# The down projection of a gated conv-MLP as seven quarter products per pair of contraction chunks, in a hybrid decoder layer on one core

## The chip, the core and the metric

The kernel runs on one core of a Trainium2 chip. The metric is the device time of one execution in microseconds (us); the median of three runs of the kernel before is 1024.78 us, the lowest 1024.64 and the highest 1025.79. The engines are named as in the profile: PE is TensorE (PEld its weight load), DVE is VectorE, ACT is ScalarE, POOL is GpSimd, SP is SyncE, which issues most transfers.

## The reference, cut to what matters

One decoder layer on 512 tokens of width 1024, in float32: a recurrent mixer and an attention mixer, merged and added to the residual stream, then a gated conv-MLP. The change is in the last line, the product with `w_down` (3072 x 1024).

```python
D_MODEL, SEQ = 1024, 512
D_FF, FFN_CONV_W = 3 * D_MODEL, 3
...
        x = x + (jax.nn.sigmoid(mg_rnn) * y_rnn + jax.nn.sigmoid(mg_attn) * y_attn) @ w_out
        up = causal_dwconv(rms_norm(x, norm2_g) @ w_up, ffn_conv_w, ffn_conv_b)
        gate, val = jnp.split(up, 2, axis=-1)
        x = x + (jax.nn.gelu(gate) * val) @ w_down
```

## The kernel before

Activations lie with the channels on the 128 partitions and the 512 tokens along the free axis. Every operand of a product is split in two, a rounded high part and the remainder as low part, and each product is three matmuls: high by high, high by low, low by high. For a weight tile of 128 x 1024, `_wprep` (line 141) issues the load into `wraw` on SP, lets ACT round it into `whi` (line 169) and DVE subtract to get `wlo` (line 177); while the attention heads run (`pool_lo`), POOL does that subtraction instead, in four pieces of 256 columns (line 174). `PLAN` lists all weight tiles in the order of their use, and `w` (line 194) prepares up to `ahead` further ones; `whi` and `wlo` have three buffers each.

The order of TensorE's work is written out by hand in the attention heads and in the MLP; what the other engines do is put in order by the scheduler, as their inputs and buffers are expected to come free.

The MLP is `ffn` (line 1255). Its up projection has 2 x 24 chunks of 128 channels. The first `NPL` = 6 pairs (a gate chunk and a value chunk) are plain products (`plain`). The other 18 are done as two-by-two blocks with seven quarter products instead of eight (`seed`, line 1329, and `rest`, line 1350): each quarter product `prod` (line 1320) is 4 x 3 matmuls with 256 columns. The sums of activation blocks are made once (`prep`); the sums of weight blocks are made in DRAM by `sums` (line 1223): SP copies blocks of the weights into a DRAM tile `ws`, and three transfers that add to what is there, issued on POOL's queue (line 1237), form the sums. `_wprep` moves `sums` on by a step each time that the position in `PLAN` has grown by the step in `SUM_RATE`, so this work is spread over the whole program. A chunk pair ends with the convolution (`conv`: one ACT operation and two on DVE), the Gelu on ACT, and the product of gate and value on POOL (`gated`, line 1278), which gives one of 24 chunks of `f`, 128 x 512.

The down projection is `down` (line 1383). For each of the 24 chunks k, `get` (line 1389) prepares the weight tile 128 x 1024 and splits the chunk of `f` into `fh` and `fl`; then, for each of the eight output blocks m, `mm3` (line 203) does three matmuls with 512 columns into the block's PSUM bank. The last two chunks are done block by block, with the residual added on DVE and the block stored as it is ready; the last block in two halves (line 1423 and 1424). It uses no POOL instruction and no weight sum.

Of the kernel before, what the change touches and what calls it, by code (L numbers as in the profile page):

```python
# [74 lines left out]
def weight_plan():  # L75
# [23 lines left out]
    p += [("dn", c, 1024) for c in range(24)]  # L99
# [21 lines left out]
class Kern:  # L121
# [18 lines left out]

    def _wprep(self, i, rp=None, pri=None):
# [3 lines left out]
        if name == "w2":  # L145

            raw = self.ea.tile([128, n], F32, name="w2r")
            hi, lo = (self.wp.tile([128, 1024], F32R, name=t, bufs=3) for t in ("whi", "wlo"))
        else:
            raw, hi, lo = self.wtiles(rp or more, more is None)  # L150
        w = self.a["w"][i, :, :n]
        if name in ("u1", "u2", "u3"):
            while self.sum_done < c:
# [14 lines left out]
        with self.tc.high_priority(self.wpri if pri is None else pri):  # L168
            self.last_hi = nc.scalar.copy(hi[:, :n], raw[:, :n])  # L169
            if self.pool_lo and (name, c) not in DVE_LO:  # L170
# [1052 lines left out]
    def sums(self):  # L1223
# [12 lines left out]
        def add(j, o, src):  # L1236
            nc.gpsimd.dma_start(self.ws[j][o], src, accum_op=ALU.add, max_dma_last_dim=8192)  # L1237
# [16 lines left out]

    def ffn(self):
# [27 lines left out]
        ff.tile([128, 8], F32, name="opad")  # L1283

        def op(name, src):
            SB[name] = [ff.tile([128, 4, 256], F32R, name=name + h) for h in ("h", "l")]
# [86 lines left out]
        ff.tile([128, 56], F32, name="fpad")  # L1373
        with self.tc.tile_pool(name="fd", bufs=1, reuse_waits="tile") as fd:
            self.rp2 = fd
            part = seed(NPL)
# [4 lines left out]
            self.down(fd, fs)

    def down(self, fd, fs):

        nc = self.nc
        ps = [self.ps.tile([128, S], F32, name="mm", bufs=self.mmb) for _ in range(7)]
        ps.append(self.ps.tile([128, S], F32, name="misc"))
        ops = {}
        def get(k):
            w = self.w("dn", k, 2 if k < 2 else 1)  # L1390
            h, l = (fd.tile([128, S], F32R, name=n, bufs=4) for n in ("fh", "fl"))
            nc.scalar.copy(h, fs(k))

            with self.tc.issue_after(self.last_sum.ins):
                nc.vector.tensor_sub(l, fs(k), h.bitcast(F32))
            ops[k] = (w, (h, l))

        def mm(m, k, c=slice(0, S)):
            w, x = ops[k]
            self.mm3(ps[m][:, c], w, slice(128 * m, 128 * m + 128), [t[:, c] for t in x], k == 0, k == FC - 1 and c.stop == S)  # L1400


        get(0)
        get(1)
        for ms in (range(0, 4), range(4, 8)):
            for k in range(2):
                for m in ms:
                    mm(m, k)
        for k in range(2, FC - DLAST):
            get(k)  # L1410
            for m in range(8):
                mm(m, k)
        for k in range(FC - DLAST, FC):
            get(k)
# [173 lines left out]
```

## Time and profile before

| what | value |
|---|---|
| runs | 1024.64, 1024.78, 1025.79 us |
| span of the profiled execution | 1024.1 us |
| attention heads, 75 to 350 us | PE busy 271.67 of 275, POOL 109.65, DMA share 0.47 |
| quarter products of the up projection, 713 to 889 us | PE and PEld busy 176.00 of 176, DVE 147.70, POOL 26.07, DMA share 0.67 |
| down projection, 889 to 1020 us | PE 131.00 of 131, PEld 108.72, DVE 49.31, ACT 36.06, POOL 2.90, DMA share 0.28 |

The time of the profiled execution itself is not given beside its span. The span goes from its first to its last instruction; the runs of the same kernel take 0.5 to 1.7 us more. Busy shares count an instruction from its start to its modelled end; matmuls overlap one another, so a rate of matmuls is read from the distance between their starts. An instruction of DVE or POOL that waits for a memory port is shown as running: its duration then is longer than that of its like.

### The profile page before, as it was taken

To read this page: it belongs to the slowest core of one execution; us is meant where nothing else is said; L and a number is where in the kernel's file an instruction comes from. 1 tells how busy PE (TensorE), PEld (TensorE's weight loads), DVE (VectorE), ACT (ScalarE), POOL (GpSimd) and SP (SyncE) were. 2 spreads that over 40 slices of the span, in tenths; PEclk is the share of its full clock that TensorE was granted. 3 is DMA by queue.
4 is the path that set the end of the run, shared out by engine and by line. 5 is a ranking of instruction groups with operands and counts; after the bars stand their busy time and mean duration, and the time that the engine had idled before them with its cause. 6 is when DMAs were issued, how large, how long until landed. Compare 5 with 4: busy or idle time off the path is not lost.

```text
span 1024.1 us, 15686 instructions
## 1 busy us (share of the span) xinstructions
PE 1013.5 (99%) x5663; PEld 882.2 (86%) x5663; DVE 750.7 (73%) x1443; ACT 615.3 (60%) x1023; POOL 243.8 (24%) x316
## 2 busy tenths in 40 slices
PE   9999999999999999999999999999999999999998
PEld 7888888988878888888888888888999999988887
DVE  6868879788878687679598564599788888933333
ACT  6466776868777663588788533365566666533320
POOL 0155334234433300342332014222211111100000
PEclk9999999999999999999999999999999999999999
DMA  7523453454545567765432987656966566632312
GB/s 252 112 89 105 124 124 116 120 120 109 145 103 150 144 218 220 218 199 165 138 92 88 291 234 208 173 151 209 266 207 200 176 194 192 200 102 85 102 62 82
DMA packets 63166, 160.88 MB, mean 157 GB/s; under 512 B 16299, under 2 KB 17963, under 8 KB 60208
## 3 DMA queue, kind: packets, MB, share of 16 engines
q1 hardware_dynamic: 57040, 137.92, 40.5%
q0 software_dynamic: 5904, 21.81, 12.6%
q8 instruction: 44, 0.72, 0.3%
q14 instruction: 34, 0.28, 0.1%
q10 hardware_dynamic: 144, 0.15, 0.0%
HBM read 150.63 MB, written 44.04 MB: 190 GB/s over the span
## 4 chain that ended last, share of the span: by engine, by line
PE 85%; DVE 8%; ACT 4%; issue 1%; DMA 1%; POOL 0%; SPq 0%; DVEq 0%; ACTq 0%
PE mm L206 16%; PE mm L207 16%; PE mm L208 16%; PE mm L1325 6%; PE mm L1326 6%; PE mm L1327 6%; PE O L916 4%; PE T L925 3%; PE S L885 1%; PE S L886 1%; PE v L767 1%; ACT s L896 1%; PE mm L1173 1%; PE em L382 1%; PE em L206 1%
## 5 line engine op out<-in xcount | busy, mean ns | idle before, releaser
L169 ACT CAST whi<-wraw 128x1024 fp32r<-128x1024 f32 (+2 forms) x202 | 203.3, 1006 | 223.9 <-PE misc L207 76.9
L177 DVE TENSOR_TENSOR wlo<-wraw,whi 128x1024 fp32r<-128x1024 f32 (+2 forms) x169 | 196.2, 1161 | 131.5 <-ACT whi L169 131.3
L206 PE MATMUL mm<-xh,whi 128*128 128x512 f32 x456 | 178.7, 392 | 0.0
L208 PE MATMUL mm<-xh,wlo 128*128 128x512 f32 x456 | 178.4, 391 | 0.0
L207 PE MATMUL mm<-xl,whi 128*128 128x512 f32 x456 | 178.2, 391 | 0.0
L174 POOL TENSOR_TENSOR wlo<-wraw,whi 128x256 fp32r<-128x256 f32 (+1 forms) x131 | 95.3, 781 | 131.9 <-ACT whi L169 110.6
L208 PEld LDWEIGHTS mm<-xh,wlo 128*128 128x128 f32 x456 | 85.6, 188 | 18.6
L206 PEld LDWEIGHTS mm<-xh,whi 128*128 128x128 f32 x456 | 85.6, 188 | 16.7
L207 PEld LDWEIGHTS mm<-xl,whi 128*128 128x128 f32 x456 | 85.6, 188 | 16.7
L896 ACT ACTIVATE s<-s,bs,rq 128x128 f32<-128x128 f32 (+3 forms) x128 | 82.5, 648 | 19.1 <-DVE bs L893 19.1
L232 DVE TENSOR_TENSOR ptl<-T,pth 128x512 fp32r<-128x512 f32 x80 | 55.1, 688 | 17.9 <-ACT pth L231 17.0
L207 PE MATMUL mm<-fl,whi 128*128 128x512 f32 x168 | 65.4, 389 | 0.0
L206 PE MATMUL mm<-fh,whi 128*128 128x512 f32 x168 | 65.4, 389 | 0.0
L208 PE MATMUL mm<-fh,wlo 128*128 128x512 f32 x168 | 65.4, 389 | 0.0
L231 ACT CAST pth<-T 128x512 fp32r<-128x512 f32 x80 | 46.3, 583 | 28.9 <-PE T L925 28.2
L889 DVE CUSTOM_DVE_ANT_0 s<-S,cc 128x128 f32<-128x128 f32 (+3 forms) x128 | 58.0, 482 | 2.2 <-PE S L886 1.7
L1237 POOL DMA_DIRECT2D ws<-ws x36 | 28.5, 792 | 121.7 <-DMA ws<-in_wi 44.7
L925 PE MATMUL T<-cc,s 128*128 128x128 f32 x320 | 48.2, 273 | 0.6 <-DVE s L901 0.6
L925 PEld LDWEIGHTS T<-cc,s 128*128 128x128 f32 x320 | 39.5, 140 | 10.1 <-DVE s L901 0.8
L1269 DVE SCALAR_TENSOR_TENSOR y<-mm,pp,y 128x511 f32<-128x511 f32 (+1 forms) x60 | 44.4, 744 | 0.1
L916 PE MATMUL O<-pth,v 128*128 128x512 f32 (+3 forms) x128 | 42.9, 353 | 1.2 <-ACT pth L231 1.1
L901 DVE TENSOR_SCALAR s<-s,sm 128x128 f32<-128x128 f32 (+3 forms) x105 | 41.6, 442 | 1.1
(405 smaller groups left out, 2634.0 us busy)
## 6 DMA issues: line engine op xcount, KB each, us to landing
wraw<-in_w SPq DMA_DIRECT2D x126, 512.0 KB, 3.6
ws<-in_wi SPq DMA_DIRECT2D x36, 512.0 KB, 5.1
wraw<-ws SPq DMA_DIRECT2D x72, 256.0 KB, 3.2
wraw<-in_w SPq DMA_DIRECT2D x54, 256.0 KB, 3.2
ws<-in_wa POOLq DMA_DIRECT2D x18, 512.0 KB, 6.0
ws<-ws POOLq DMA_DIRECT2D x36, 256.0 KB, 4.6
xr<-in_x SPq DMA_DIRECT2D x16, 256.0 KB, 4.4
x<-in_x SPq DMA_DIRECT2D x8, 256.0 KB, 4.3
```

The costliest lines, as they stand in the source:

```text
L169: self.last_hi = nc.scalar.copy(hi[:, :n], raw[:, :n])
L174: nc.gpsimd.tensor_sub(lo[:, e], raw[:, e], hi[:, e].bitcast(F32))
L177: nc.vector.tensor_sub(lo[:, :e], raw[:, :e], hi[:, :e].bitcast(F32))
L206: nc.tensor.matmul(ps, wh, xh, start=first, stop=False)
L207: nc.tensor.matmul(ps, wh, xl, start=False, stop=False)
L208: nc.tensor.matmul(ps, wl, xh, start=False, stop=last)
L896: self.last_exp = nc.scalar.activation(s[t, x], s[t, x], AF.Exp, bias=bs[:, x, t:t + 1], scale=rq[:, t], accum_out=sm[:, x, t:t + 1])
L916: nc.tensor.matmul(O[:, q0:S], lhsT, r, start=first[0], stop=(last and n == len(rhs) - 1))
L925: nc.tensor.transpose(T[:, off:off + 128], s[i, x][:, 128 * j:128 * j + 128], self.ident)
L1325: nc.tensor.matmul(ps, w[0][:, c], xh, start=start and k == 0, stop=False, skip_group_check=True)
L1326: nc.tensor.matmul(ps, w[0][:, c], xl, start=False, stop=False, skip_group_check=True)
L1327: nc.tensor.matmul(ps, w[1][:, c], xh, start=False, stop=(k == 3), skip_group_check=True)
```

## The change

The down product is done for pairs of chunks (`pair`: k and k + 4), each a two-by-two block problem: two chunks by two halves of the 1024 outputs for the weights, two chunks by two halves of the 512 tokens for `f`. Seven quarter products instead of eight are accumulated over all twelve pairs, in two phases. In phase one (`one`, weight tiles d1 and d2) four of the products are accumulated for all twelve pairs; then `mix` combines the PSUM banks of each group (ACT copies a bank, DVE does four additions of 256 columns); in phase two (`two`, tiles d3 and d4, the latter of 512 columns) the remaining three are added. Each quarter product of a group p of output blocks is three matmuls with 256 columns; there are four groups.

The weights of a pair need four blocks that are sums. Two of them are made in DRAM by `sums`, which gets twelve more rounds behind the old ones: one copy of 512 KB on SP and two adding transfers of 256 KB on POOL's queue each. The other two are made on POOL in SBUF (`down_sums`). The activations need two differences and sums in phase one (`down_ops`: two operations on DVE, one on POOL) and one in phase two (`down_ops2`), written over chunks of `f`. `SUM_RATE` gets smaller steps, so that sums are issued closer together. The low part of d4 is made on POOL (line 205 of the new file), the others on DVE. Buffers of the up projection's operands (`fo`) are taken over as they come free.

The diff, cut to its core:

```diff
+def pair(n):
+    k = 8 * (n // 4) + n % 4
+    return k, k + 4
-SUM_AT, SUM_RATE = 20, ((43, 1.0), (66, 2.4), (82, 16.0), (116, 2.0), (999, 3.0))
+SUM_AT, SUM_RATE = 20, ((43, 0.6), (66, 1.5), (82, 16.0), (116, 1.3), (999, 2.4))
...
-    p += [("dn", c, 1024) for c in range(24)]
+    for n in range(FC // 2):
+        p += [("d1", n, 1024), ("d2", n, 1024)]
+    for n in range(FC // 2):
+        p += [("d3", n, 1024), ("d4", n, 512)]
...
+    def dtiles(self, i):
+        if (i - WIDX[("d1", 0)]) % 4 == 3:
+            return [self.fo.tile([128, 1080 - o], F32R, name=t, tag=g)[:, 56 - o:1080 - o]
+                    for t, g, o in (("whi", "t4h", 0), ("wlo", "t4l", 56))]
+        return [self.wp.tile([128, 1024], F32R, name=t, bufs=3) for t in ("whi", "wlo")]
...
+            m = c + FC // 2 * (name == "d3")
+            if name in ("d1", "d3") and m:
+                self.down_load(m + 2)
+                self.down_sums(m + 1)
+            raw = self.dn_raw.pop((name, c))
+            hi, lo = self.dtiles(i)
...
-            if self.pool_lo and (name, c) not in DVE_LO:
+            if (self.pool_lo and (name, c) not in DVE_LO) or name == "d4":
...
+        for n in range(N + 2):
+            if n < N:
+                self.ds[n] = self.drp.tile([64, 2048], F32, name=f"dn{n}")
+                nc.sync.dma_start(self.ds[n], a["wd"][n])
+                yield
+            if 0 <= n - 1 < N:
+                add(self.ds[n - 1][0:32], a["we"][n - 1])
+            if 0 <= n - 2 < N:
+                add(self.ds[n - 2][32:64], self.ds[n - 2][0:32])
+            yield
...
+    def down_load(self, m):
...
+            if late:
+                dma(g[:, 512:], w[i, :, 512:1024])
+                dma(g[:, 0:512], self.dsum(n, 1))
+                dma(s[:, 0:512], w[i + 1, :, 0:512])
+            else:
+                dma(g[:, 0:512], w[i, :, 0:512])
+                dma(s[:, 0:512], w[i, :, 512:1024])
+                dma(g[:, 512:], self.dsum(n, 1))
+                dma(s[:, 512:], self.dsum(n, 0))
...
+    def down_sums(self, m):
...
+            if late:
+                self.nc.gpsimd.tensor_tensor(g[:, 0:512], g[:, 0:512], g[:, 512:], ALU.add)
+            else:
+                self.nc.gpsimd.tensor_tensor(s[:, 0:512], s[:, 0:512], g[:, 0:512], ALU.add)
...
+    def down_ops(self, n, fs):
...
+        v.tensor_sub(t[:, 0], b11, b12)
+        nc.gpsimd.tensor_tensor(t[:, 1], b22, b12, ALU.subtract)
+        v.scalar_tensor_tensor(b12, t[:, 0], -1.0, b22, ALU.mult, ALU.subtract)
+        self.split(flat(h[:, 0:2]), flat(l[:, 0:2]), f1)
+        self.split(flat(h[:, 2:4]), flat(l[:, 2:4]), flat(t))
...
+    def down_ops2(self, n, fs):
...
+        v.scalar_tensor_tensor(f1[:, 0:256], f1[:, 256:512], -1.0, f2[:, 0:256], ALU.mult, ALU.subtract)
+        self.split(flat(h[:, 0:2]), flat(l[:, 0:2]), f2)
+        self.split(h[:, 2], l[:, 2], f1[:, 0:256])
...
+            nc.tensor.matmul(ps, w[0][:, c], x[0][:, i], start=start, stop=False, skip_group_check=True)
+            nc.tensor.matmul(ps, w[0][:, c], x[1][:, i], start=False, stop=False, skip_group_check=True)
+            nc.tensor.matmul(ps, w[1][:, c], x[0][:, i], start=False, stop=stop, skip_group_check=True)
...
+        get1(0)
+        for p, which in ((0, "ac"), (1, "ac"), (2, "c"), (0, "de"), (1, "de"), (2, "ade")):
+            one(p, 0, which)
+        get1(1)
+        for p, n in ((0, 1), (1, 1), (3, 0), (2, 1), (3, 1)):
+            one(p, n)
+        for n in range(2, N):
+            get1(n)
+            for p in range(4):
+                one(p, n)
+                if n == N - 1:
+                    mix(p)
...
+        for p in range(3):
+            two(p, N - 1)
+            store(p, 0, (slice(0, S),))
+            store(p, 1, (slice(0, S),))
+            if p < 2:
+                two(p + 2, N - 2)
+        for s in "cda":
+            two(3, N - 1, s)
+            if s == "c":
+                store(3, 1, (slice(0, S),))
+        store(3, 0, (hi, lo))
```

How the change moves instructions is shown at three places. TensorE's order is the same up to the first matmul of the down product, and everything behind that is new. In the middle of the down product, DVE's order before is this: `wlo` is the low part of a weight tile, `fl` that of a chunk of `f`, for one chunk after the other.

```order
L177 TENSOR_TENSOR wlo_10177<-wraw_10175,whi_10176 128x1024
L1395 TENSOR_TENSOR fl_10250<-fxl_7329,fh_10249 128x512
L177 TENSOR_TENSOR wlo_10211<-wraw_10209,whi_10210 128x1024
L1395 TENSOR_TENSOR fl_10284<-fxl_7329,fh_10283 128x512
L177 TENSOR_TENSOR wlo_10245<-wraw_10243,whi_10244 128x1024
```

DVE's order now, for one pair in the middle of phase one (`dg` and `ds` are the raw tiles d1 and d2, `dt` the differences of blocks of `f`, `dl` the low parts of the activation operands):

```order
L208 TENSOR_TENSOR wlo_10159<-dg_10005,whi_10158 128x1024
L208 TENSOR_TENSOR wlo_10163<-ds_10006,whi_10162 128x1024
L263 TENSOR_TENSOR dl_10289<-fxh_7388,dh_10288 128x512
L263 TENSOR_TENSOR dl_10289<-dt_10287,dh_10288 128x512
L1501 SCALAR_TENSOR_TENSOR fxh_7388<-fxh_7388 128x256
L1487 TENSOR_TENSOR dt_10505<-fxl_7389 128x256
L1489 SCALAR_TENSOR_TENSOR fxl_7389<-dt_10505,fxl_7389 128x256
```

A pair now has two weight tiles, two splits and three small operations, one of which (line 1501) belongs to phase two. Each of the seven has two inputs, both in SBUF.

POOL's last instructions before are the products of gate and value of the last chunks:

```order
L1278 TENSOR_TENSOR fxl_7329<-y_9240,y_9245 128x512
L1278 TENSOR_TENSOR fxl_7329<-y_9370,y_9375 128x512
L1278 TENSOR_TENSOR fxl_7329<-y_9500,y_9505 128x512
L1278 TENSOR_TENSOR fxl_7329<-y_9629,y_9634 128x512
L1278 TENSOR_TENSOR fxl_7329<-y_9687,y_9692 128x512
```

Now, from the product of chunk 21 on, POOL's order runs like this, with the weight sum `ds` (line 1329) and the difference `dt` (line 1488) of the first pairs among them:

```order
L1354 TENSOR_TENSOR fxl_7389<-y_9560,y_9565 128x512
L1329 TENSOR_TENSOR ds_9780<-ds_9780,dg_9779 128x512
L1488 TENSOR_TENSOR dt_9922<-f0_6931 128x256
L1488 TENSOR_TENSOR dt_10068<-fxh_7388 128x256
L1354 TENSOR_TENSOR fxl_7389<-y_9689,y_9694 128x512
L1329 TENSOR_TENSOR ds_9797<-ds_9797,dg_9796 128x512
L1354 TENSOR_TENSOR fxl_7389<-y_9755,y_9760 128x512
L1329 TENSOR_TENSOR ds_9848<-ds_9848,dg_9847 128x512
L1488 TENSOR_TENSOR dt_10141<-fxh_7388 128x256
```

Behind that come one `ds` and one `dt` per pair, and in phase two one sum of 512 columns (line 1327) and two low parts of 256 columns (line 205) per pair.

In the attention heads POOL also issues the adding transfers. Before, between low parts of weights (line 174) and operations of the compressed attention (lines 834 to 865), where `ws` is the DRAM tile of the sums:

```order
L1237 DMA ws6_1326<-ws6_1326 32x2048 x2
L174 TENSOR_TENSOR wlo_1481<-wraw_1479,whi_1480 128x256 x4
L1237 DMA ws7_1761<-in_wa 64x2048
L174 TENSOR_TENSOR wlo_1599<-wraw_1597,whi_1598 128x256 x4
L174 TENSOR_TENSOR wlo_1759<-wraw_1757,whi_1758 128x256 x4
L1237 DMA ws7_1761<-ws7_1761 32x2048 x2
L174 TENSOR_TENSOR wlo_1936<-wraw_1934,whi_1935 128x256 x4
L1237 DMA ws8_2356<-in_wa 64x2048
```

The same stretch of POOL's order now:

```order
L1268 DMA ws6_1326<-ws6_1326 32x2048
L1268 DMA ws7_1601<-in_wa 64x2048
L1268 DMA ws6_1326<-ws6_1326 32x2048
L205 TENSOR_TENSOR wlo_1481<-wraw_1479,whi_1480 128x256 x4
L1268 DMA ws7_1601<-ws7_1601 32x2048 x2
L205 TENSOR_TENSOR wlo_1599<-wraw_1597,whi_1598 128x256 x4
L205 TENSOR_TENSOR wlo_1761<-wraw_1759,whi_1760 128x256 x4
L1268 DMA ws8_1940<-in_wa 64x2048
L1268 DMA ws8_1940<-ws8_1940 32x2048
L205 TENSOR_TENSOR wlo_1937<-wraw_1935,whi_1936 128x256 x4
L1268 DMA ws8_1940<-ws8_1940 32x2048
```

Among the weights of the heads, POOL issues adds for 13 chunks where it did for 8 before; the twelve new rounds stand between the recurrent mixer and the first quarter products of the up projection.

More of the change, by code (lines that the diff above doesn't have):

```diff
@@ L1255, in ffn @@
+    def down_sums(self, m):
+        n, late = m % (FC // 2), m // (FC // 2)
+        if late < 2:
+            g, s = (self.dn_raw[(k, n)] for k in (("d3", "d4") if late else ("d1", "d2")))
+            if late:
+                self.nc.gpsimd.tensor_tensor(g[:, 0:512], g[:, 0:512], g[:, 512:], ALU.add)
+            else:
+                self.nc.gpsimd.tensor_tensor(s[:, 0:512], s[:, 0:512], g[:, 0:512], ALU.add)
     def ffn(self):
@@ L1281, in ffn @@
         SB = {}
[L1283 to L1286 removed]
+        FO = ExitStack()
+        tp = lambda name, **kw: self.tc.tile_pool(name=name, bufs=1, reuse_waits="tile", **kw)
+        for _ in range(4):
+            ff.tile([128, S], F32, name="y", bufs=4)
+        fo = self.fo = FO.enter_context(tp("fo"))
+        fo.tile([128, 8], F32, name="opad")
+        def op(name, src):
+            if name == "t4":
+                sizes = ((name + "h", 1080, 0), (name + "l", 1032, 8))
+                SB[name] = [fo.tile([128, n], F32R, name=t)[:, o:o + 1024].rearrange("p (k c) -> p k c", k=4)
+                            for t, n, o in sizes]
+            else:
+                SB[name] = [fo.tile([128, 4, 256], F32R, name=name + h) for h in ("h", "l")]
             self.split(*SB[name], src)
@@ L1359, in rest @@
             gated(j, yg, conv(r1, FC + j, True))
-        with self.tc.tile_pool(name="xt", bufs=1, reuse_waits="tile") as xt:
+        with tp("xt", side="right") as xt:
             x = xt.tile([128, KO, S], F32, name="xs")
@@ L1378, in ffn @@
                 nx = seed(j + 1) if j + 1 < FC else None
+                if j == FC - 3:
+                    for _ in self.sum_steps:
+                        pass
+                    self.down_load(0)
+                if nx is None:
+                    self.down_sums(0)
+                    first = self.down_ops(0, fs)
+                    fd.tile([128, 56], F32, name="fdpad")
                 rest(j, *part)
                 part = nx
[L1381 to L1414, printed above, removed]
-        for m in range(8):
@@ new lines, in ffn @@
+            self.down(fs, first)
+        FO.close()
+    def down_ops(self, n, fs):
+        nc, v = self.nc, self.nc.vector
+        k1, k2 = pair(n)
+        f1, f2 = fs(k1), fs(k2)
+        b11, b12, b22 = f1[:, 0:256], f1[:, 256:512], f2[:, 256:512]
+        t = self.dtile(n, [128, 2, 256], F32, "dt", ("t2l", "b22l"))
+        h, l = (self.dtile(n, [128, 4, 256], F32R, x, y) for x, y in (("dh", ("t1h", "b21h")), ("dl", ("t1l", "b21l"))))
+        flat = lambda x: x.rearrange("p a c -> p (a c)")
+        v.tensor_sub(t[:, 0], b11, b12)
[3 more added lines that the diff above has]
+        self.split(flat(h[:, 2:4]), flat(l[:, 2:4]), flat(t))
+        return h, l
@@ new lines, in down @@
+        get2(1)
+        for p, n in ((0, 1), (3, 0), (1, 1), (2, 1), (3, 1)):
+            two(p, n)
+        for n in range(2, N - 2):
+            get2(n)
+            for p in range(4):
+                two(p, n)
+        get2(N - 2)
+        two(0, N - 2)
+        two(1, N - 2)
+        get2(N - 1)
+        for p in range(3):
+            two(p, N - 1)
[3 more added lines that the diff above has]
+                two(p + 2, N - 2)
@@ L1525, in lay_out @@
         wa[j] = np.stack([v[:, 0:4], v[:, 4:8]])
+    wd = np.asarray(i["w_down"]).reshape(FC, 128, 2, 512)
+    ks = np.array([pair(n) for n in range(FC // 2)])
+    wd, we = np.stack([wd[ks[:, 0], :, 1], wd[ks[:, 0], :, 0]], 1), wd[ks[:, 1], :, 1]
     pp = np.zeros((128, NP_), f)
```

124 lines of the change are left out of this document (105 added, 19 removed).

## Prediction, made before the change was run

> **What bounds the kernel now.** First the busy times on the page, then the same by stage: the heads, the quarter products of the up projection, the down projection. The columns of a stage are busy time (and instructions) of PE, PEld, DVE, ACT and POOL, granted clock, DMA share and GB/s.
>
> ```profile
> PE 1013.5 (99%) x5663; PEld 882.2 (86%) x5663; DVE 750.7 (73%) x1443; ACT 615.3 (60%) x1023; POOL 243.8 (24%) x316
> 75.00:350.00 275.00, 271.67 (x1581) 235.60 (x1580) 227.75 (x688) 201.74 (x460) 109.65 (x148) 1.00 0.47 126
> 713.00:889.00 176.00, 176.00 (x1510) 176.00 (x1509) 147.70 (x216) 110.88 (x143) 26.07 (x22) 1.00 0.67 205
> 889.00:1020.00 131.00, 131.00 (x587) 108.72 (x585) 49.31 (x57) 36.06 (x47) 2.90 (x2) 1.00 0.28 92
> ```
>
> PE has no gap in the down projection and runs at full clock; everything else there is far from busy. So the stage is worth its matmuls, and the rate of matmuls is read from PE's timeline, by the distance of starts:
>
> ```profile
> 888.30 0.28 PE L1325 MATMUL mm<-t4h,whi 128*128 128x256 f32 x1
> ...
> 889.00 0.28 PE L1325 MATMUL mm<-t4h,whi 128*128 128x256 f32 x1
> ...
> 889.35 0.39 PE L206 MATMUL mm<-fh,whi 128*128 128x512 f32 x1
> ...
> 985.25 0.39 PE L206 MATMUL mm<-fh,whi 128*128 128x512 f32 x1
> ...
> 999.53 0.39 PE L206 MATMUL mm<-fh,whi 128*128 128x512 f32 x1
> ...
> 1019.89 0.28 PE L208 MATMUL misc<-fh,wlo 128*128 128x256 f32 x1
> ```
>
> Six matmuls of 256 columns take 0.70 us, 0.1167 each; 63 of 512 take 14.28, 0.2267 each. A half-size matmul is a little more than half as long.
>
> **The matmuls.** Removed are 570 of 512 columns and 12 of 256: 129.2 + 1.4 = 130.6 us, which fits the start at 889.35 and the last matmul at 1019.89. Added are 12 pairs x 4 groups x 7 products x 3 = 1008 of 256 columns: 117.6. The term is **-13.0 us**; at half of 0.2267 it would be 16.3. Phase one is 12 x 48 matmuls, 5.60 us a pair; phase two 12 x 36, 4.20 a pair. All else is what keeps PE from this pace.
>
> **The work beside it.** Prices on DVE come from its timeline at the end of the up projection and, for 256 columns, from the group of its additions there; POOL's from the products of gate and value and from a low part in the heads:
>
> ```profile
> L1344 DVE TENSOR_TENSOR ac<-mm,ad 128x256 f32<-128x256 f32 x9 | 3.8, 427 | 4.1 <-PE mm L1327 4.1
> 876.97 1.22 DVE L177 TENSOR_TENSOR wlo<-wraw,whi 128x1024 fp32r<-128x1024 f32 x1
> 878.10 0.75 DVE L1269 SCALAR_TENSOR_TENSOR y<-mm,pp,y 128x510 f32<-128x510 f32 x1
> 878.76 0.74 DVE L1269 SCALAR_TENSOR_TENSOR y<-mm,npw,y 128x511 f32<-128x511 f32 x1
> 879.42 0.68 DVE L177 TENSOR_TENSOR wlo<-wraw,whi 128x512 fp32r<-128x512 f32 x1
> 880.02 0.74 DVE L1269 SCALAR_TENSOR_TENSOR y<-mm,npw,y 128x510 f32<-128x510 f32 x1
> L1278 POOL TENSOR_TENSOR fxh<-y x8: 1297/1300/1300, 753.7 to 822.1; 128x512 f32<-128x512 f32 x8
> 353.25 2.82 POOL L174 TENSOR_TENSOR wlo<-wraw,whi 128x256 fp32r<-128x256 f32 x4 [5.49 <-ACT whi L169]
> 900.23 1.05 ACT L169 CAST whi<-wraw 128x1024 fp32r<-128x1024 f32 x1 [1.15 <-PE misc L207]
> 901.18 0.62 ACT L1392 CAST fh<-f 128x512 fp32r<-128x512 f32 x1
> ```
>
> In a row without waits an operation costs DVE the distance to the next start: 1.13 for 1024 columns, 0.60 for 512, 0.66 for a tap of the convolution; for 256, recorded at 0.43, I take 0.34, the same 0.09 less. On POOL 512 columns take 1.30 and 256 take 2.82 / 4 = 0.71.
>
> A pair of phase one needs, on DVE, 2 x 1.13 + 2 x 0.60 + 3 x 0.34 = 4.48 us of the 5.60; on ACT, 2 x 1.05 + 2 x 0.62 = 3.34; on POOL, 1.30 + 0.71 = 2.01. One of phase two: DVE 1.13 + 0.60 + 0.34 = 2.07 of the 4.20, POOL 1.30 + 2 x 0.71 = 2.72, ACT less than in phase one. Loads are 1 MB in 5.60 us and 0.75 MB in 4.20, about 187 GB/s, where the up projection moves 205 at a share of 0.67. The buffers of raw tiles let a load start two pairs ahead of its sum. Each engine alone keeps up; I cost loads and ACT at nothing.
>
> **DVE and POOL together.** They do not run freely beside each other. Six places of the timelines of POOL and DVE, and the spread of one small DVE operation (min/median/max in ns):
>
> ```profile
> 703.98 1.29 POOL L1278 TENSOR_TENSOR f<-y 128x512 f32<-128x512 f32 x1 [7.73 <-DVE y L1269]
> 704.34 2.02 DVE L177 TENSOR_TENSOR wlo<-wraw,whi 128x1024 fp32r<-128x1024 f32 x1
> 693.37 2.14 POOL L1278 TENSOR_TENSOR f<-y 128x512 f32<-128x512 f32 x1 [4.18 <-DVE y L1269]
> 693.14 1.21 DVE L177 TENSOR_TENSOR wlo<-wraw,whi 128x1024 fp32r<-128x1024 f32 x1
> 276.24 3.11 POOL L174 TENSOR_TENSOR wlo<-wraw,whi 128x256 fp32r<-128x256 f32 x4
> 276.30 3.08 DVE L893 SCALAR_TENSOR_TENSOR bs<-mx,rq 128x4 f32<-128x4 f32 x1
> L893 DVE SCALAR_TENSOR_TENSOR bs<-mx,rq x32: 153/166/3080, 88.9 to 344.5; 128x4 f32<-128x4 f32 x32
> 871.10 1.30 POOL L1278 TENSOR_TENSOR fxl<-y 128x512 f32<-128x512 f32 x1 [8.50 <-DVE y L1269]
> 871.42 0.43 DVE L1344 TENSOR_TENSOR ac<-mm,ad 128x256 f32<-128x256 f32 x1 [0.46 <-PE mm L1327]
> ```
>
> A DVE subtraction of two SBUF tiles that starts inside a POOL product ends 1.09 us after it (706.36 against 705.27), 2.02 instead of 1.22. The other way round POOL waits: it ends 1.16 after DVE (695.51 against 694.35). A DVE operation of 0.17 us lasts 3.08 through four of POOL's. An addition with one input in PSUM is not slowed at all. So operations with two inputs in SBUF take turns with POOL, and every steady operation of the new down product is such a one. A POOL operation between two of DVE puts them apart by 1.16 + 1.09 - 1.13 = 1.12 instead of its 1.30; for 256 columns I take 0.18 less too, 0.53.
>
> Phase one then needs 4.48 + 1.12 + 0.53 = 6.13 of 5.60 a pair: 0.53 too much in pairs 3 to 9, 3.7 us; pairs 10 and 11 have one small operation left and fit. That is a bound on DVE's pace and it moves PE, which waits for `wlo` of the next pair. Between all turns hidden (0) and every operation at its recorded length (2 x 1.22 + 2 x 0.68 + 3 x 0.43 + 2.01 = 7.10, 1.50 too much, 10.5 us) I take 3.7, as its rows show the turns themselves.
>
> The start: DVE's order from the first addition of the last `seed` (in this trace at 881.22) to the low part of pair 2's second tile has 7 operations of 1.13, 5 of 0.60, 8 taps of 0.66 and 9 of 0.34: 19.3 us, ending at 900.5. PE wants that part two pairs, two products and two matmuls into the stage: 889.35 + 11.2 + 0.7 + 0.2 = 901.5. One us is to spare, and POOL has seven of 512 columns and three of 256 in that time, 9.4 us in turns; 12 of DVE's operations read PSUM and take 6.6 us in which they cost nothing. Between 0 and 8.4 I take **2.3**: a third of POOL's turns delaying DVE, less the spare. Phase one: 3.7 + 2.3 = **+6.0**.
>
> Phase two needs 2.07 + 1.12 + 2 x 0.71 - 0.18 = 4.43 of 4.20: 0.23 x 11 = 2.5. The sums there are made up to two pairs ahead, so the first pairs don't feel it; I take half, **+1.2** (0 to 9.4: at recorded lengths 1.22 + 0.68 + 0.43 + 2.72 = 5.05, 0.85 too much in each).
>
> The change of phase: `mix` of the last group can't start before that group's products; its five steps, 0.6 on ACT and four of 0.34 to 0.43, stand in DVE's queue behind the other groups' and a `wlo`. PE does three groups of pair 0 and one of pair 1 ahead of it, 4.2 us. DVE's queue for that time has some 4.8: **+0.7** (0 to 2).
>
> The end, before, and a stretch of the table by stage in which the transfers run fast:
>
> ```profile
> 0.00:25.00 25.00, 23.48 (x94) 18.77 (x94) 17.43 (x31) 17.68 (x29) 0.20 (x4) 1.00 0.72 248
> 1018.77 0.69 DVE L1423 TENSOR_TENSOR y<-mm,xn 128x512 f32<-128x512 f32 x1 [0.67 <-PE mm L208]
> 1020.20 0.76 DVE L1423 TENSOR_TENSOR y<-misc,xn 128x256 f32<-128x256 f32 x2 [0.74 <-PE misc L208]
> ```
>
> DVE ends 0.8 us after PE. Now the last 18 matmuls, 2.1 us, finish four blocks, 3 x 0.60 + 2 x 0.34 = 2.5 us on DVE starting 0.9 us into them: 1.2 us after PE, 0.4 later. Three blocks of 256 KB and two halves are stored 0.6 us apart instead of 1.36; at 248 GB/s one takes 1.06, a queue of about 0.7. **+1.1** (0.4 to 2).
>
> The adds in DRAM: they touch PE only where POOL or the transfers run out. In the heads:
>
> ```profile
> L1237 POOL DMA_DIRECT2D ws<-ws x16 | 12.6, 786 | 46.4 <-DMA ws<-ws 15.6 <-DMA ws<-in_wi 11.9 <-DMA ws<-in_wa 7.7
> L1237 POOL DMA_DIRECT2D ws<-in_wa x8 | 6.9, 860 | 29.5 <-DMA ws<-in_wi 23.7 <-PE T L925 5.8
> POOL wlo L174 <- ACT whi L169: 63.0, 17, 14.0
> ```
>
> 24 adds cost POOL (19.5 + 75.9) / 24 = 4.0 us each, waits included; 15 more cost 60. POOL has 63 us there in which it waits for ACT to round a weight: that hides them, just. I take 0 (-1 to +6).
>
> **Sum.** Against the span: 1024.1 - 13.0 + 6.0 + 1.2 + 0.7 + 1.1 = 1020.1. The median run lies 0.7 above the span: **1020.8 us**.
>
> **Rivals.** (1) The turns cost nothing: POOL's operations fall into gaps of DVE, or DVE goes first and the sums are early enough. For: DVE has 1.1 us free in each pair of 5.60, and sums stand a pair ahead. Against: 4.48 and 1.65 don't fit into 5.60. Time: 1024.8 - 13.0 + 0.7 + 1.1 = 1013.6, up to 1016 with some start. 0.28.
>
> (2) Slower: DVE and POOL hold the port for the whole recorded length of each operation. By the sums above: start 8.4, phase one 10.5, phase two 9.4, with 1.8 for change and end: 1024.8 - 13.0 + 30.1 = 1042. It turns the gain into a loss once start and turns take more than 11.2 us together. For: the operation that waited 3.08 us through four of POOL's, so a run of one engine isn't broken into. Against: 1.09 and 1.16 after the other's end are less than 1.22 and 1.30. 0.10. The Trainium skill, SBUF — State Buffer, "Who interferes with whom", has this rule: a VectorE instruction with two SBUF inputs and a GpSimd instruction that reads SBUF exclude each other through a shared read port, for the whole instruction. By that rule no part of an operation overlaps, and the down product comes out at this rival's price; the trace agrees on who waits, and shows 0.13 us less of each wait.
>
> (3) POOL's queue in the heads runs full: the 60 us of waits don't fall where POOL is idle, and a low part comes late by up to one add, 4.0 us. One such wait takes the forecast's whole gain of 4.0, and that is the point from which it decides; fifteen more adds with 1.5 such waits in all cost 6: 1026.8. Against: PE loses 3.3 of 275 us in the stage now. 0.10.
>
> **How the numbers follow.** The forecast has 0.52. A measurement of this kernel can tell about 0.2%, 2.1 us, from no change: 1022.7 to 1026.8. Of the forecast's 0.52, 0.38 lie below, 0.13 within, 0.01 above; rival 1 is faster; rival 2 slower; rival 3 half within, half above. Faster 0.66, same 0.18, slower 0.16. The range reaches down to rival 1, a little under it for a DVE that ends no later, and up past rival 3: 1012.5 to 1028; rival 2 and some edges are left out.
>
> **What would show it.** Right: matmuls 0.1167 apart; DVE subtractions in the down product of 1.5 to 2.3 us beside POOL's sums; waits of PE for `wlo` of 5 to 8 us by the end of phase one, fewer in phase two. Rival 1: DVE at its old lengths and PE without gaps. Rival 2: DVE and POOL busy nearly all of the stage, and PE waiting in every pair. Rival 3: PE waits for POOL's low parts between 75 and 350 us. The forecast is wrong if PE's waits in the down product are under 3 or over 12 us, or lie before 889 us.

## The result, and the profile after

The changed kernel takes 1037.64 us (median of 4 runs, 1034.42 to 1041.22), the kernel before 1025.28 (4 runs, 1024.64 to 1026.74): ratio 1.012, interval 1.009 to 1.0151. It is slower, by 0.9 to 1.5%, and outside the range that was forecast. The profiled execution took 1034.42 us, with a span of 1032.6.

The page's busy times and the table by stage (heads, quarter products of the up projection, phase one and phase two of the new down product; columns as before):

```profile
PE 1009.4 (98%) x6089; PEld 896.8 (87%) x6089; DVE 823.3 (80%) x1531; ACT 644.8 (62%) x1075; POOL 350.7 (34%) x400
75.00:350.00 275.00, 271.24 (x1573) 234.63 (x1572) 226.96 (x690) 202.13 (x461) 118.19 (x160) 1.00 0.61 160
713.00:893.00 180.00, 180.00 (x1528) 179.34 (x1528) 154.76 (x224) 113.20 (x146) 34.94 (x28) 1.00 0.64 200
893.00:972.00 79.00, 74.55 (x598) 73.17 (x597) 75.25 (x97) 41.58 (x58) 44.21 (x24) 0.96 0.49 157
972.00:1028.00 56.00, 51.11 (x415) 50.02 (x413) 43.75 (x43) 24.37 (x41) 38.16 (x31) 0.97 0.42 138
```

In phase one DVE is now busy in 75.25 of 79.00 us, in a stage where it had been idle most of the time; PE has gaps, and in both phases the mean granted clock is below 1.00. PE's timeline shows where the down product begins, its longest wait and what follows that, and its last matmul:

```profile
893.01 0.28 PE L1521 MATMUL mm<-dh,whi 128*128 128x256 f32 x1
...
917.77 0.28 PE L1522 MATMUL mm<-dl,whi 128*128 128x256 f32 x1
920.89 0.58 PE L1523 MATMUL mm<-dh,wlo 128*128 128x256 f32 x1 [2.85 <-DVE wlo L208]
921.27 0.42 PE L1521 MATMUL mm<-dh,whi 128*128 128x256 f32 x1
921.49 0.42 PE L1522 MATMUL mm<-dl,whi 128*128 128x256 f32 x1
...
926.82 0.41 PE L1523 MATMUL misc<-dh,wlo 128*128 128x256 f32 x1
...
1027.67 0.28 PE L1523 MATMUL mm<-dh,wlo 128*128 128x256 f32 x1
```

The first down matmul starts at 893.01, where it had been 889.35: 3.7 us are lost ahead of the changed product. From the first to the last it takes 134.7 us instead of 130.5. After the last, 4.9 us remain instead of 4.2. That is the whole difference of the spans: 3.7 + 4.1 + 0.7 = 8.5.

The 1008 matmuls at 0.1167 us would take 117.5 to the start of the last, so 17.2 us are lost inside. By phase, each distance of starts less 0.1167 summed: 9.5 us in phase one, 7.6 in phase two with the change of phase. A new item is in both. Between 921.27 and 926.82 the starts are 0.2135 us apart, not 0.1167, and the granted clock of that stretch is half:

```profile
920.30:927.10 6.80, 6.21 (x29) 6.21 (x30) 6.80 (x12) 0.63 (x2) 1.04 (x2) 0.50 0.46 157
```

So a wait of 2.85 us is followed by 28 matmuls at half speed, 2.7 us more. A second one follows the longest wait of phase two and costs 1.6. These are the waits of PE from 713 us on, all of them in the down product:

```profile
PE mm L1523 <- DVE wlo L208: 4.6, 5, 2.9
PE mm L1523 <- POOL wlo L205: 3.9, 2, 2.6
PE misc L1521 <- DVE misc L1553: 0.7, 1, 0.7
```

Three places explain most of it. The **first** is the wait of 2.85 us. POOL's last product of gate and value, 1.30 us of work, is recorded with 10.84; then DVE, which until 911.90 had run one two-input operation behind the other, waits 3.13 us for POOL's activation difference, which had stood behind that product. POOL's row, then DVE's:

```profile
902.22 10.84 POOL L1354 TENSOR_TENSOR fxl<-y 128x512 f32<-128x512 f32 x1 [0.37 <-ACT y L1444]
```

```profile
911.22 0.68 DVE L263 TENSOR_TENSOR dl<-dt,dh 128x512 fp32r<-128x512 f32 x1
915.03 1.50 DVE L1489 SCALAR_TENSOR_TENSOR fxh<-dt,fxh 128x256 f32<-128x256 f32 x1 [3.13 <-POOL dt L1488]
```

After the wait DVE meets the turns of POOL that had piled up: its four operations of 256 columns from 915.03 on take 4.60 us up to the next low part, where four distances of 0.34 make 1.36. The low parts of the first weight tile show the pace of DVE over the whole phase; these are those of the first, the fifth and the ninth pair:

```profile
892.85 1.22 DVE L208 TENSOR_TENSOR wlo<-dg,whi 128x1024 fp32r<-128x1024 f32 x1
...
919.63 1.21 DVE L208 TENSOR_TENSOR wlo<-dg,whi 128x1024 fp32r<-128x1024 f32 x1
...
945.09 1.22 DVE L208 TENSOR_TENSOR wlo<-dg,whi 128x1024 fp32r<-128x1024 f32 x1
```

The first four pairs take DVE 26.8 us and the next four 25.5, where PE needs 22.4 for four; the three rows after that take 4.9 us each and fit. PE is 5.2 us behind its pace when the wait of 2.85 us ends, and loses 4.2 more in the pairs from there on, half clock included.

The **second** is at the beginning of phase two. POOL makes the sums (L1327) and the low parts of the fourth weight tile (L205) in turn; SyncE's queue issues the loads (L1313 the fourth tile's, L1311 and L1312 the third's). First POOL's timeline, then the queue's:

```profile
964.97 1.98 POOL L1327 TENSOR_TENSOR dg<-dg 128x512 f32<-128x512 f32 x1 [1.63 <-DMA dg<-dn]
966.90 2.09 POOL L205 TENSOR_TENSOR wlo<-ds,whi 128x256 fp32r<-128x256 f32 x2
973.61 1.81 POOL L1327 TENSOR_TENSOR dg<-dg 128x512 f32<-128x512 f32 x1 [4.61 <-DMA dg<-dn]
975.37 1.60 POOL L205 TENSOR_TENSOR wlo<-ds,whi 128x256 fp32r<-128x256 f32 x2
981.44 1.27 POOL L1327 TENSOR_TENSOR dg<-dg 128x512 f32<-128x512 f32 x1 [4.47 <-DMA dg<-dn]
```

```profile
962.22 7.13 SPq L1313 DMA_DIRECT2D ds<-in_w  x2
969.40 0.42 SPq L1311 DMA_DIRECT2D dg<-in_w  x1
969.87 0.43 SPq L1312 DMA_DIRECT2D dg<-dn  x1
977.00 0.33 SPq L1313 DMA_DIRECT2D ds<-in_w  x1
977.37 0.43 SPq L1311 DMA_DIRECT2D dg<-in_w  x1
```

The low part ends at 968.99 and frees a buffer; only then the next fourth tile's load is issued, and behind it on the queue, at 969.40 and 969.87, the third's; POOL's sum starts when that has landed, at 973.61, and the low part after it at 975.37. This goes round once in 8 us, while PE does a pair in 4.2, and PE's two waits for POOL are the result.

The **third** lies outside the down product, in the recurrence. PE waits there for the load of a tile `st` that POOL issues, and POOL had been kept by two of the accumulating adds, which now stand closer together. PE's row, then POOL's:

```profile
436.85 0.70 PE L1110 MATMUL mm<-st,whi 126*128 126x512 f32 x2 [1.53 <-DMA st<-xcl]
437.39 0.40 PE L237 MATMUL mm<-xh,whi 128*128 128x512 f32 x1
```

```profile
422.96 0.79 POOL L1268 DMA_DIRECT2D ws<-ws x1 [4.86 <-DMA ws<-in_wa]
...
428.67 0.82 POOL L1268 DMA_DIRECT2D ws<-ws x1 [2.71 <-DMA ws<-ws]
...
430.23 0.82 POOL L1092 DMA_DIRECT2D st<-xcl  x1
```

Compared matmul by matmul with the kernel before, PE is 0.5 us behind at 350 us, 2.3 after this wait, and 3.5 from 611 us on, where a weight's load is late.

### The profile page after: what moved, and what is told of

Same layout as the page of the kernel before. It is cut to its first block, busy times and chain, and to the rows that moved or that the text cites. A ratio compares the mean times of both kernels' runs of the same rounds, so it can differ in the third digit from the quotient of the medians.

```text
span 1032.6 us, 17032 instructions
## 1 busy us (share of the span) xinstructions
PE 1009.4 (98%) x6089; PEld 896.8 (87%) x6089; DVE 823.3 (80%) x1531; ACT 644.8 (62%) x1075; POOL 350.7 (34%) x400
## 5 line engine op out<-in xcount | busy, mean ns | idle before, releaser
L200 ACT CAST whi<-wraw 128x1024 fp32r<-128x1024 f32 (+3 forms) x178 | 177.7, 998 | 143.5 <-PE mm L1412 55.3
L208 DVE TENSOR_TENSOR wlo<-wraw,whi 128x1024 fp32r<-128x1024 f32 (+2 forms) x145 | 167.8, 1157 | 58.0 <-ACT whi L200 58.0
L205 POOL TENSOR_TENSOR wlo<-wraw,whi 128x256 fp32r<-128x256 f32 (+1 forms) x131 | 95.7, 813 | 82.2 <-ACT whi L200 71.7
L1523 PE MATMUL mm<-dh,wlo 128*128 128x256 f32 x300 | 86.8, 289 | 8.6 <-DVE wlo L208 4.6
L1521 PE MATMUL mm<-dh,whi 128*128 128x256 f32 x300 | 85.6, 285 | 0.0
L1522 PE MATMUL mm<-dl,whi 128*128 128x256 f32 x300 | 85.3, 284 | 0.0
L1523 PEld LDWEIGHTS mm<-dh,wlo 128*128 128x128 f32 x300 | 58.3, 194 | 10.5 <-DVE wlo L208 6.0
L1521 PEld LDWEIGHTS mm<-dh,whi 128*128 128x128 f32 x300 | 58.3, 194 | 0.2 <-ACT y L1444 0.2
L1522 PEld LDWEIGHTS mm<-dl,whi 128*128 128x128 f32 x300 | 58.2, 194 | 0.0
L200 ACT CAST whi<-dg 128x1024 fp32r<-128x1024 f32 x24 | 25.2, 1052 | 50.4 <-PE mm L1522 25.6
```

What stands on the lines that cost most here:

```text
L205: nc.gpsimd.tensor_sub(lo[:, e], raw[:, e], hi[:, e].bitcast(F32))
L208: nc.vector.tensor_sub(lo[:, :e], raw[:, :e], hi[:, :e].bitcast(F32))
L1521: nc.tensor.matmul(ps, w[0][:, c], x[0][:, i], start=start, stop=False, skip_group_check=True)
L1522: nc.tensor.matmul(ps, w[0][:, c], x[1][:, i], start=False, stop=False, skip_group_check=True)
L1523: nc.tensor.matmul(ps, w[1][:, c], x[0][:, i], start=False, stop=stop, skip_group_check=True)
```

## Experiments

The theory after the result had an **order** part (A: the three places are chains of waits, each to be undone by moving one operation) and its rival was **pace** (B: DVE has more to do beside POOL than fits, wherever a wait shows). All times are against the kernel before on the same chip (medians 1024.4 to 1025.8). "Lost" is what PE loses in a phase against 0.1167 a matmul, from the profile:

| kernel | time, us | ratio to before (interval) | down begins | lost in phase one | lost in phase two |
|---|---|---|---|---|---|
| changed kernel | 1037.64 | 1.012 (1.009 to 1.0151) | 893.0 | 9.5 | 7.6 |
| e1_gate_dve | 1037.0 | 1.0113 (1.0096 to 1.0129) | 897.5 | 8.6 | 7.1 |
| e2_d4_dve | 1032.84 | 1.0096 (1.0066 to 1.0125) | 893.3 | 10.3 | 2.0 |
| e3_both | 1029.49 | 1.0048 (1.0031 to 1.0064) | 890.9 | 9.5 | 2.1 |
| b1_rounds_only | 1029.37 | 1.0055 (1.0026 to 1.0084) | 894.6 | none | none |
| f1_no_sums1 | 1024.17 | 0.9974 (0.9956 to 0.9993) | 891.5 | 3.1 | 1.7 |
| e4_add_for_product | 1037.61 (one run) | | 896.5 | 10.0 | 7.0 |
| f3_rounds_later | 1030.99 | 1.0041 (1.0025 to 1.0057) | 895.4 | 9.5 | 2.2 |
| f4_late_steps2 | 1028.73 | 1.0029 (1.0018 to 1.0041) | 896.0 | 6.4 | 2.4 |
| f5_rounds_moved | 1027.12 | 1.0004 (0.9989 to 1.002) | 893.4 | 7.3 | 2.9 |
| f6_sum_by_dma | 1019.95 | 0.9948 (0.9929 to 0.9968) | 889.9 | 2.5 | 1.6 |

**The last gated product on DVE** (e1_gate_dve).

```diff
-            nc.gpsimd.tensor_mul(fs(j), yg, yv)
+            (nc.vector if j == FC - 1 else nc.gpsimd).tensor_mul(fs(j), yg, yv)
```

> The product of gate and value of the last chunk goes from GpSimd to VectorE. Theory A (order): in the changed kernel this product stood 9.55 us behind an unbroken row of VectorE operations, the activation difference of the fourth pair stood behind it on GpSimd, VectorE then waited 3.13 us for that, and TensorE waited 2.85 us and ran 6.8 us at half clock; all of it goes, about 6 us less than the changed kernel: 1028 to 1032 us against 1034 to 1041. Theory B (pace): VectorE has too much to do beside GpSimd's turns, whatever the order; it gets 0.6 us more, and the time stays or grows by 0.6. Under A no GpSimd operation of the down product lasts over 4 us and the first long wait of TensorE, at about 918 us, is under 1 us; under B the wait is where it was or a pair later.

The order theory's forecast failed here. The 2.85 us wait and its half clock are gone, but phase one loses 8.6 us instead of 9.5, in more and shorter waits, the longest 1.3. The repair was not clean, though: another POOL operation took the product's place behind the row of DVE operations, a sum:

```profile
908.09 8.70 POOL L1329 TENSOR_TENSOR ds<-ds,dg 128x512 f32<-128x512 f32 x1 [2.50 <-DVE dt L1487]
```

What sets the phase is seen in one whole row of DVE in it, from the low part of one pair's first tile to that of the next:

```profile
929.12 1.21 DVE L208 TENSOR_TENSOR wlo<-dg,whi 128x1024 fp32r<-128x1024 f32 x1
930.25 2.31 DVE L208 TENSOR_TENSOR wlo<-ds,whi 128x1024 fp32r<-128x1024 f32 x1
932.49 0.68 DVE L263 TENSOR_TENSOR dl<-fxh,dh 128x512 fp32r<-128x512 f32 x1
933.09 0.68 DVE L263 TENSOR_TENSOR dl<-dt,dh 128x512 fp32r<-128x512 f32 x1
933.69 0.41 DVE L1501 SCALAR_TENSOR_TENSOR fxh<-fxh 128x256 f32<-128x256 f32 x1
934.03 0.95 DVE L1487 TENSOR_TENSOR dt<-fxl 128x256 f32<-128x256 f32 x1
934.90 0.41 DVE L1501 SCALAR_TENSOR_TENSOR fxh<-fxh 128x256 f32<-128x256 f32 x1
935.24 0.41 DVE L1489 SCALAR_TENSOR_TENSOR fxl<-dt,fxl 128x256 f32<-128x256 f32 x1
935.57 1.21 DVE L208 TENSOR_TENSOR wlo<-dg,whi 128x1024 fp32r<-128x1024 f32 x1
```

No gap stands in it, and it takes 6.45 us where PE needs 5.60. The second low part is put off by 1.11 us beside POOL's sum, the difference of activations by 0.53 beside POOL's; two steps of phase two (L1501) stand in it.

**The fourth tile's low parts on DVE** (e2_d4_dve), and **both edits** (e3_both).

```diff
-            if (self.pool_lo and (name, c) not in DVE_LO) or name == "d4":
+            if (self.pool_lo and (name, c) not in DVE_LO):
```

> The low parts of the fourth weight tile (phase two) are made by VectorE in one operation of 512 columns instead of two of 256 on GpSimd. Theory A (a loop of waits): in phase two the load of a fourth tile waits for GpSimd's low part three pairs back, the loads of the third tile stand behind it on SyncE's queue, GpSimd's sum waits for those, and the next low part stands behind the sum; about 8 us a pair against TensorE's 4.2. Without it TensorE's waits of 1.37 and 2.58 us for GpSimd's low parts and 3.4 us at half clock go, some 6 us less than the changed kernel. Theory B (pace): VectorE gets 12 x 0.60 = 7.2 us more and is the limit; no gain, up to 3 us longer. Phase one stays as it is under both.

Here order was right: phase two loses 2.0 us instead of 7.6, PE no longer waits for POOL, and phase one loses 10.3, no less than before. DVE carries the 7.2 us more, since a pair of phase two leaves it room.

> Both edits of the two kernels before together: the last gated product and the low parts of the fourth tile on VectorE. Theory A: the gains add, 10 to 13 us less than the changed kernel, 1023 to 1027 us, so within 0.2% of the kernel before; the down product takes 121 to 124 us from its first matmul to its last, with no half clock. Theory B: within 3 us of the changed kernel, with TensorE's waits for VectorE's low parts in most pairs.

It is 1029.49 us, between the two expectations. Of the 7.3 us by which its span is shorter than the changed kernel's, 5.5 are phase two's, and 2.1 lie ahead of the down product. There is no stretch at half clock in its down product, yet phase one loses 9.5 us as before. That speaks for DVE as the pace, which caught up while PE was slow; that the 2.7 us at half clock cost nothing there is argued, not shown. For the product on DVE also brings a wait of its own: in the third pair PE waits 1.1 us for the low part of an activation operand, in all seven kernels that have this edit and in none of the other three of the table with the new down product.

**The rounds alone** (b1_rounds_only): the kernel before with `sums` and its table from the changed kernel.

> The kernel before, with its own down product, plus only the rounds of copies and accumulating transfers for the down weights and the denser table of rounds; what they make isn't read. In the changed kernel the down product began 3.7 us later than before. Theory A: the extra rounds hold up weights' loads and GpSimd's queue: this kernel is 2 to 4.5 us slower than the kernel before, with waits of TensorE near 434 us and 610 us. Theory B: the delay came with the other parts (pools, tiles, the order around the up projection): within 0.7 us of the kernel before.

1.0055 of the time before, so 2.7 to 8.6 us, with the old down product at its old 130.5 us. The price is paid in the recurrence:

```profile
PE mm L1085 <- DMA st<-xcl: 3.6, 1, 3.6
```

This wait stands in all seven profiles that have the entry 1.5 ahead of the recurrence (1.5 to 3.6 us), and in none of the five with 2.4 (the kernel before among them). The wait near 610 us, which was expected too, did not come in this one.

**The sums of phase one left out** (f1_no_sums1: the kernel of e3_both without POOL's twelve sums, so that the second weight tile holds one of its two terms).

```diff
-            else:
+            elif m < 0:
                 self.nc.gpsimd.tensor_tensor(s[:, 0:512], s[:, 0:512], g[:, 0:512], ALU.add)
```

> The kernel with both edits on VectorE, and GpSimd's twelve sums of phase one left out (so the second weight tile holds one of its two terms): what the sums cost VectorE by their turns on the read port. Theory A (turns): with the sums VectorE's row of a pair takes 6.3 us against TensorE's 5.6 and TensorE waits in most pairs of phase one; without them the row takes about 5.2, the waits for low parts in pairs 2 to 11 go, and the down product takes 123 to 125 us instead of 129.1. Theory B (the waits come from casts, loads or the order of the row): the down product stays above 127.5 us, with the waits in the same pairs.

The down product takes 122.3 us instead of the 129.1 of e3_both, and 6.4 of the difference are gained in phase one. Twelve sums cost PE 0.5 us each, though no wait of PE in phase one names a sum.

**An addition in place of the product** (e4_add_for_product: the changed kernel, with POOL's last product of gate and value an addition of the same tiles).

```diff
+            nc.gpsimd.tensor_tensor(fs(j), yg, yv, ALU.add if j == FC - 1 else ALU.mult)
```

> The changed kernel with one instruction altered: the last product of gate and value on GpSimd is an addition of the same two tiles (so the last chunk holds another value). In the traces GpSimd's products waited through a whole unbroken row of VectorE operations, 9.55 us the last of them, where its sums and differences got in after one. If that hangs on what the instruction does, the addition is recorded at under 2.6 us here; if it hangs on the row of VectorE operations it stands beside, the addition is recorded at 8 to 11 us like the product. The whole time says nothing here: 1033 to 1041 us under both.

```profile
L1354 POOL TENSOR_TENSOR fxl<-y x8: 1298/1302/10835, 839.0 to 905.3; 128x512 f32<-128x512 f32 x8
```

10.84 us again: it is the place, not the operation. There a POOL operation waits for the end of a row of 14 DVE operations; in the steady part of phase one it comes in after one of them. What makes the two differ stays open.

**The rounds after the recurrence** (f3_rounds_later: e3_both with another table).

```diff
-SUM_AT, SUM_RATE = 20, ((43, 0.6), (66, 1.5), (82, 16.0), (116, 1.3), (999, 2.4))
+SUM_AT, SUM_RATE = 20, ((43, 1.0), (66, 2.4), (82, 16.0), (116, 1.5), (999, 1.4))
```

> Both edits on VectorE, and the table of rounds as in the kernel before up to the recurrence (1.0, 2.4, 16.0), then denser (1.5, 1.4 in place of 1.3, 2.4), so that the extra rounds run after the loads of the recurrence. Theory A (the accumulating transfers on GpSimd's queue hold up the loads of the recurrence's tiles, and the wait of 1.5 to 3.6 us there trips the clock): the wait for that load is gone, the down product begins within 1 us of the kernel before, 1025 to 1027 us, and the spread of runs falls under 4 us. Theory B (rounds cost wherever they stand): the waits move to the up projection's loads, and the time stays at 1029 to 1031.

The first half of A held (no wait for `st`), the second half is B's: PE now waits in the up projection, where it had not waited at all, and the transfers there are full. The wait, and the same stretch in the kernel before and in this one:

```profile
PE mm L1413 <- DVE wlo L208: 5.3, 6, 1.7
```

```profile
713.00:780.00 67.00, 67.00 (x576) 67.00 (x575) 54.72 (x79) 41.55 (x53) 11.78 (x11) 1.00 0.75 226
```

```profile
713.00:780.00 67.00, 63.03 (x530) 61.97 (x529) 54.31 (x77) 36.85 (x48) 20.89 (x22) 1.00 0.94 282
```

**The steps of phase two held back** (f4_late_steps2, with the table of f3_rounds_later): each L1501 from the fourth pair on is put behind the last step of the mixing.

```diff
+        with self.tc.issue_after(self.last_mix.ins) if n > 2 else nullcontext():
+            v.scalar_tensor_tensor(f1[:, 0:256], f1[:, 256:512], -1.0, f2[:, 0:256], ALU.mult, ALU.subtract)
```

> The kernel with the rounds later, and VectorE's nine activation steps of phase two from the fourth pair on are held back until the first mixing is done; they stood in phase one, one in nearly every pair. Theory A (VectorE's row is the bound of phase one): 9 x 0.33 = 3.0 us less in phase one; phase two has room for them; 2 to 3 us less than the kernel with the rounds later. Theory B: phase one's waits come from the turns at the second tile's low part alone, and phase two pays for the steps: no change within 1 us.

Phase one loses 6.4 instead of 9.5 us, 3.1 less where 9 x 0.33 = 3.0 was expected; phase two loses 0.2 more. The median is 2.3 us lower, as expected of A. DVE's row is the bound: what is taken out of it, PE gains.

**The rounds moved** (f5_rounds_moved: e3_both with the late steps and the table below) and **the sums by transfers** (f6_sum_by_dma: the same kernel, the twelve sums of phase one made by transfers).

```diff
+SUM_AT, SUM_RATE = 20, ((43, 0.6), (66, 2.4), (82, 16.0), (116, 1.5), (999, 2.4))
```

> Both edits on VectorE, the late activation steps, and the table of rounds of the changed kernel but for two entries: 2.4 in place of 1.5 ahead of the recurrence (as in the kernel before), 1.5 in place of 1.3 ahead of the up projection. Seven rounds fewer stand ahead of the recurrence and 11 in place of 2 in the up projection (where the table with 1.4 put over 30 and filled the transfers to a share of 0.94). Theory A (the load of the recurrence's tiles and a full set of transfers are two separate prices, both avoidable): no wait for that load, no half clock near 436 us, the down product begins by 891.5 and takes 126 to 127 us: 1024 to 1027 us. Theory B (a round costs some 0.4 us wherever it stands): the down product begins after 893.5 and the time stays at 1027.5 to 1030.

Not settled: the wait for `st` is gone and 1027.12 us lies at the edge of both expectations. Its down product begins at 893.4, but that of f6_sum_by_dma, with the same table, at 889.9, and whether that is the execution or the twelve sums isn't separated; the rounds' price with this table isn't known better than 0.5 to 4.0 us.

```diff
-                self.nc.gpsimd.tensor_tensor(s[:, 0:512], s[:, 0:512], g[:, 0:512], ALU.add)
+                w = self.a["w"][WIDX[("d1", n)], :, 0:512]
+                self.nc.gpsimd.dma_start(s[:, 0:512], w, accum_op=ALU.add)
```

> The kernel with the rounds moved, and the twelve sums of phase one made by accumulating transfers from DRAM onto the loaded tile instead of by GpSimd's additions; GpSimd only issues them. Theory A (the sums cost by their turns on the read port with VectorE): as in the kernel without those sums, the waits for low parts in phase one go; the down product takes 120 to 123 us, 4 to 6 us less than with the rounds moved: 1019 to 1022 us, faster than the kernel before. Theory B (a transfer that must follow a landed load, behind GpSimd's other work, comes late): ScalarE and then TensorE wait for the second tile, and the down product takes 126 us or more.

A held: 121.65 us from the first to the last down matmul, 6.0 less than with the rounds moved alone, and 1019.95 us in all, 0.3 to 0.7% under the kernel before. DVE's rows show why. These are the low parts of the first tile of the fourth and the ninth pair, first in f5_rounds_moved, with POOL's sums, then in this kernel:

```profile
907.49 1.22 DVE L208 TENSOR_TENSOR wlo<-dg,whi 128x1024 fp32r<-128x1024 f32 x1
...
943.24 1.22 DVE L208 TENSOR_TENSOR wlo<-dg,whi 128x1024 fp32r<-128x1024 f32 x1
```

```profile
903.00 1.21 DVE L208 TENSOR_TENSOR wlo<-dg,whi 128x1024 fp32r<-128x1024 f32 x1
...
934.05 1.22 DVE L208 TENSOR_TENSOR wlo<-dg,whi 128x1024 fp32r<-128x1024 f32 x1
```

Five rows of DVE take 35.75 us with POOL's sums and 31.05 without, where PE needs 28.0; phase one loses 4.8 us less. Of the 2.5 us that it still loses, 1.2 are lost at the wait in the third pair that came with the product on DVE.

The Trainium skill, SBUF — State Buffer, "Who interferes with whom", gives transfers ports of their own, apart from the engines'; these rows agree: the same sum costs DVE a turn as a POOL operation and none as a transfer.

## Why the prediction was wrong, step by step

The span is 12.5 us longer than forecast (1032.6 against 1020.1): 5.7 by phase two, 3.7 by the adds in DRAM, 3.5 by phase one, less 0.4 at the end.

- **The matmuls, -13.0: right.** At full clock they start 0.1167 us apart, and the 1008 of them make 117.5 us.
- **Phase one, +6.0: the mechanism right, the start mis-sized.** That DVE's row sets PE's pace is shown by f1_no_sums1 and f4_late_steps2, and the turns had their forecast price (1.11 and 0.53 against 1.12 and 0.53). The steady pairs were put at 3.7, and PE loses 4.2 in them: four rows of DVE are too long by 3.1 in all, with up to four steps of phase two in one row, where seven rows of 6.13 us had been forecast. The start was put at 2.3 (a third of POOL's 9.4 less the spare 1.0 gives 2.1), and PE is 5.2 behind at the fifth pair. The forecast let a third of POOL's turns delay DVE; in fact POOL was held through the row at 902 to 912 us, DVE waited 3.13 us for the difference behind the held product, and the other turns then fell together. How much of this the held operation costs was not separated, since in e1_gate_dve another one was held in its place.
- **Phase two and the change of phase, +1.9: the step that failed, and the largest, was "I cost loads and ACT at nothing".** It was argued that the buffers of raw tiles let a load start two pairs ahead of its sum. For the fourth tile a buffer is free only after POOL's low part, which stands behind a sum, which waits for loads that are queued behind the one that needs the buffer. It lost 7.6. With that loop cut (e2_d4_dve, e3_both), phase two lost 2.0 and 2.1, near the forecast's 1.9.
- **The adds in DRAM, 0: wrong, and rival 3 named the wrong place.** POOL's 63 us of waits in the heads did nearly cover them there (PE is 0.5 us behind at 350 us). But the table was made denser ahead of the recurrence as well, and there POOL issues loads that PE waits for. The profile before had those loads on POOL's queue; I counted only low parts. 3.7 us in this profile, 2.7 to 8.6 by b1_rounds_only.
- **The end, +1.1: measured +0.7.**
- **Not foreseen: the clock.** Every wait was priced at its length. In phase two a wait of 2.58 us cost 1.6 more by the half clock after it, and in the recurrence the same can follow (matmuls recorded at 0.63 us in place of 0.39 after the wait in b1_rounds_only). In phase one the half clock fell into a time when DVE was late anyway, as argued at e3_both.
- **Rival 2** gave 1042 and was near the time, but not by its cause: operations did not hold the port for their recorded lengths (a row would take 7.10 us). Start and turns came to at most 9.5 and 2.1 us, about the 11.2 from which it was to decide; what makes the kernel slower lies beyond them, in the loop (5.6) and the rounds (3.7).

Put together: 1024.1 - 13.0 + 9.5 + 7.6 + 3.7 + 0.7 = 1032.6, the span.

## What to carry to other kernels

When an engine of little load gets a full row of work, add up the whole row between two of its dues, with everything a scheduler may pull into it, and treat the sum as a pace: a wait that is removed from such a phase comes back elsewhere, as in e1_gate_dve. For each buffer of a new stream write down who frees it and what stands ahead of that operation on its engine; a load behind it on the same queue closes a loop that no engine's busy share shows. And a table that makes side work denser has to be followed through every stage that it passes, looking for loads issued from the same queue.

## What the runs showed of the hardware

Waits shorter than three microseconds can be followed by half clock, and the length of the wait alone doesn't decide. In e4_add_for_product a wait of 1.58 us was followed by a stretch at a granted clock of 0.56, while in the same run a wait of 2.85 us was not: from 920 to 935 us the granted clock is 1.00. The two rows of PE, then those of the two stretches:

```profile
923.96 0.39 PE L1523 MATMUL mm<-dh,wlo 128*128 128x256 f32 x1 [2.85 <-DVE wlo L208]
...
938.21 0.38 PE L1523 MATMUL mm<-dh,wlo 128*128 128x256 f32 x1 [1.58 <-DVE wlo L208]
```

```profile
920.00:935.00 15.00, 11.76 (x94) 10.94 (x93) 13.61 (x21) 6.89 (x10) 8.59 (x6) 1.00 0.40 137
939.60:943.00 3.40, 3.40 (x19) 3.40 (x19) 3.29 (x6) 0.00 (x0) 0.81 (x2) 0.56 0.81 289
```

The wait of 1.53 us for `st`, quoted above, was followed by matmuls of 0.40 us, as ever there. What decides isn't shown here. The Trainium skill, TensorE: Matmul & The Clock Gate, "HAM oscillation — how this bites in real kernels", sets the limit for an idle gap at about 3.4 us; here half of that was enough in one place and 2.85 us were not in another, and the measurement decides.

A POOL operation on SBUF can be held through a whole row of DVE operations (9.55 us), not only through one, and at the start of the down product this happened to a product, to an addition in its place, to a sum (recorded at 8.70 us) and in f6_sum_by_dma to a difference (7.66 us). And an accumulating transfer from DRAM onto an SBUF tile does a 256 KB sum without a turn of the port: POOL's timeline in f6_sum_by_dma records 0.88 us to issue it.
